# A 8192 x 8192 transpose: loads that split the rows of a chunk into even and odd halves

## The chip, the cores and the metric

The kernel runs on one core of one Trainium2 chip. Its time is the device time of one execution in microseconds. The time before is the median of three runs.

## The reference

```python
def setup_inputs():
    return {"x": np.random.randn(8192, 8192).astype(np.float32)}

def reference(x):
    return np.transpose(x)
```

An fp32 matrix of 268.4 MB is read once, and its transpose of the same size is written once.

## The kernel before

Each of the matrix's 8192 rows is 32 KB long. The work is cut into 128 chunks. A chunk is 128 rows by 4096 columns (`J = S * P`, 32 blocks of 128 columns), so 2 MB; the 64 chunks (`CH`) of the left half of the columns come first, then the 64 of the right half. Partition p of the chunk's buffer holds row p of the chunk, 16 KB of it in one piece.

One chunk passes through four stages:

- **Load.** `load(t)` issues one transfer from `x` into one of three buffers (`ins`, `NIN = 3`). The first three loads are issued on the SP queue, all later ones on the ACT queue. A load adds 16 to `s_ld[k]` of its buffer when it has landed.
- **Transposes.** `transposes(k)` on TensorE does 32 transposes of 128 x 128 against `ident`, with the data as the stationary side, into the two PSUM tensors `pss[0]` and `pss[1]` (16 blocks each). A group q of four transposes takes every fourth column of 512, so that four neighbouring output rows come to lie in one partition. TensorE begins a chunk when `s_ld[k]` is 18: 16 from the load and one from each copying engine, which says that the previous chunk's PSUM is free. It signals `s_pe` four times a chunk.
- **Copies.** ScalarE (ACT) copies `pss[0]` and VectorE (DVE) copies `pss[1]` into `regs`, a ring of nine regions in SBUF. A region collects the same q over eight successive chunks (`W = 8`), which makes 1024 neighbouring columns of the output, 4 KB for each output row.
- **Store.** When a region is full, `store(q, e, t)` writes it to `out` in one transfer of 2 MB, on the ACT queue. In the steady state one region closes per chunk. Before a region is used again, the copying engine waits for its last store (`s_st[r]`).

The order on ACT is written out by hand in the loop over `chunks`: the copies of chunk t, then a wait for the first signal of TensorE in chunk t+1 (by then both engines' copies of t are done), then the store that closed in t, then `load(t + NIN)`. So the store of t and the load of t+3 are issued one after the other, shortly after the load of t+1 has landed. The copies of chunk t+1 on ACT stand behind them.

`wide_dma` builds a transfer directly from the two access patterns that it is given, so that the source and the destination may be cut into pieces differently (stores read 16 KB from a partition and write it as four rows of 4 KB). `physical` writes the pattern down as it stands, and puts a count of 1 into a pattern of two dimensions. `dma_start` is the ordinary way, used for the loads and for the first transfer of a queue.

The diff touches the making of `ident` on GpSimd (POOL), `load`, one wait of VectorE, and one wait of TensorE.

Of the kernel before, what the change touches and what calls it, by code (L numbers as in the profile page):

```python
# [8 lines left out]
def physical(ap):  # L9


    t = ap.tensor
    dims = [list(d) for d in ap.ap]
    if len(dims) == 2:
        dims.insert(1, [dims[1][1], 1])
    return mybir.PhysicalAccessPattern(
        ap=dims,
        offset=ap.offset,
        dtype=ap.dtype,
        memref=t.name,  # L20
        memsetref=t.name + "_set",
    )


def wide_dma(nc, eng, queue, out, in_):


    return eng.add_instruction(
        mybir.InstDMACopy(
            mode="Copy",  # L30
            name=nc.get_next_instruction_name(),
            engine=eng.engine,
            ins=[physical(in_)],
            outs=[physical(out)],
            queue=queue,
        )
    )
# [3 lines left out]
def kernel(  # L41
# [13 lines left out]
    nc = tc.nc  # L55
    P = 128
# [8 lines left out]
    NIN = 3  # L65
    NREG = 9
    CH = N // P
    J = S * P

    with tc.tile_critical():  # L70
        nc.alloc_sbuf_tensor("pad", [P, 32], dt)
        ident = nc.alloc_sbuf_tensor("ident", [P, P], dt).ap()
        ins = [nc.alloc_sbuf_tensor(f"in{k}", [P, J], dt).ap() for k in range(NIN)]
        SIZE = B * W * P
# [4 lines left out]
        s_id = nc.alloc_semaphore("s_id")  # L79
        s_ld = [nc.alloc_semaphore(f"s_ld{k}") for k in range(NIN)]  # L80
# [3 lines left out]

        nc.gpsimd.memset(ident, 0.0).then_inc(s_id, 1)  # L85
        nc.gpsimd.wait_ge(s_id, 1)
        nc.gpsimd.affine_select(  # L87
            out=ident,
            in_=ident,
            compare_op=mybir.AluOpType.not_equal,  # L90
            fill=1.0,
            base=0,
            pattern=[[-1, P]],
            channel_multiplier=1,
        ).then_inc(s_id, 1)
        nc.vector.sem_inc(s_ld[0], 1)
        nc.scalar.sem_inc(s_ld[0], 1)

        chunks = [(s, c) for s in range(M // J) for c in range(CH)]

        def load(t):
            s, c = chunks[t]
            (nc.sync if t < NIN else nc.scalar).dma_start(
                out=ins[t % NIN], in_=x[c * P:(c + 1) * P, s * J:(s + 1) * J]
            ).then_inc(s_ld[t % NIN], 16)

# [16 lines left out]
        T = len(chunks)  # L125
        assert T % NIN == NIN - 1
        pe = [nc.tensor.engine]
        nc.tensor.wait_ge(s_id, 2)

        turn = nc.alloc_registers("turn", engines=pe)  # L130
        nc.regs_mov(turn, 0)
# [11 lines left out]
        for t in range(NIN):  # L143
            load(t)
# [9 lines left out]
        def store(q, e, t):  # L154
# [7 lines left out]
            for s, a, z in parts:  # L162
                rows = (z - a) * P
                j0 = s * J + q * B * P
                dst = out[j0:j0 + B * P, a * P:a * P + rows]
# [19 lines left out]
        for t, (s, c) in enumerate(chunks):  # L185
            closed = []
            for e in range(2):
                eng = (nc.scalar, nc.vector)[e]
# [4 lines left out]
                for q in range(e * NH, (e + 1) * NH):  # L193
# [14 lines left out]
                    base = r * SIZE + B * P * sum(z - a for _, a, z in parts[:k])  # L208
# [52 lines left out]
            if t + NIN < T:  # L261
                if not closed:
                    nc.scalar.wait_ge(s_pe, (t + 1) * NH)
                load(t + NIN)
# [32 lines left out]
```

## Time and profile before

| | |
|---|---|
| time, median of 3 runs | 1261.94 us (1261.61 to 1261.95) |
| span of the profiled execution | 1260.4 us |
| moved | 536.95 MB, 426 GB/s over the span |
| PE busy | 739.0 us (59%), 4096 matmuls |
| DVE busy | 302.0 us (24%) |
| ACT busy | 253.5 us (20%) |
| transfers | 128 loads of 2 MB, 142 stores of 256 KB to 2 MB |

The profile is one execution on the chip. Busy times are those of the compute engines; the issue of a transfer isn't counted as busy. The span is also shown in 40 equal slices: a digit is the busy share of a slice in tenths (9 is 90% or more), the row DMA is the mean busy share of the 16 DMA engines, and the row GB/s is what they moved. The rows on queues give packets, MB, and the time that the packets took as a share of 16 engines' span: q10 is ACT's queue, q1 is SP's. In the groups, the part behind the bar is busy time and the mean of one instruction, then the idle time ahead of them and what ended it.

### The profile page before, as it was taken

The numbers are of one execution on the slowest core, as the hardware profiler recorded it, in microseconds if no ns is written. First come the engines' busy times: TensorE is split into PE (matmuls) and PEld (weight loads), VectorE is DVE, ScalarE is ACT, GpSimd is POOL, SyncE is SP. The second block draws the span as 40 slices with busy tenths as digits, with TensorE's granted clock in tenths as the row PEclk, the third lists the DMA queues.
The fourth block names the chain that finished last, engine by engine and source line by source line (L and its number), as shares of the span: only waits on it lengthen the run. The fifth ranks groups of instructions, "written<-read, shape, count | busy, mean of one in ns | idle before, by whom it ended". The sixth has DMA issues, their size and how long they took to land. (4 is left out here: it accounts for less than half of the span.)

```text
span 1260.4 us, 9367 instructions
## 1 busy us (share of the span) xinstructions
PE 739.0 (59%) x4096; PEld 718.4 (57%) x4096; DVE 302.0 (24%) x250; ACT 253.5 (20%) x257; POOL 0.7 (0%) x6
## 2 busy tenths in 40 slices
PE   5656556565566655565556656566565655665561
PEld 5556556565556655565555656565565655665561
DVE  2322222222222222222222222222222222222220
ACT  3212211122111211122111211121111211121110
POOL 0000000000000000000000000000000000000000
PEclk9886876868777777778687786867777687777776
DMA  9999999999999999999999999999999999999998
GB/s 383 429 422 426 425 430 431 426 431 431 427 430 431 428 428 431 428 429 432 427 422 426 429 429 425 431 429 428 430 428 428 431 428 429 429 429 429 429 431 376
DMA packets 39271, 536.95 MB, mean 426 GB/s; under 512 B 4320, under 2 KB 4832, under 8 KB 6240
## 3 DMA queue, kind: packets, MB, share of 16 engines
q10 hardware_dynamic: 38832, 530.60, 99.0%
q1 hardware_dynamic: 432, 6.29, 1.2%
q14 instruction: 6, 0.05, 0.0%
q8 instruction: 1, 0.02, 0.0%
HBM read 268.44 MB, written 268.44 MB: 426 GB/s over the span
## 5 line engine op out<-in xcount | busy, mean ns | idle before, releaser
L117 PE MATMUL ps<-ident,in 128*128 128x128 f32 x4096 | 739.0, 362 | 493.5 <-PEq L113 493.5
L117 PEld LDWEIGHTS ps<-ident,in 128*128 128x128 f32 x4096 | 718.4, 220 | 513.9 <-issue 513.9
L241 DVE COPY regs<-ps 128x512 f32<-128x512 f32 (+3 forms) x250 | 302.0, 1246 | 932.1 <-PE ps L117 932.1
L241 ACT COPY regs<-ps 128x512 f32<-128x512 f32 (+3 forms) x256 | 252.2, 1016 | 978.8 <-PE ps L117 760.8
L241 ACT ACT_TABLE_LOAD x1 | 1.3, 1283 | 1.0 <-SPq L70 1.0
L87 POOL TENSOR_SCALAR_AFFINE_SELECT ident<-ident 128x128 f32<-128x128 f32 x1 | 0.3, 293 | 0.2 <-POOL ident L85 0.2
L85 POOL MEMSET ident<- 128x128 f32 x1 | 0.2, 204 | 0.5 <-SPq L70 0.5
L281 POOL MEMSET const-bfloat16-1.0<- 128x1 bf16 x1 | 0.1, 102 | 0.0
L281 POOL MEMSET const-uint8-127<- 128x1 uint8 x1 | 0.1, 102 | 0.0
L281 POOL MEMSET const-float32-0.0<- 128x1 f32 x1 | 0.1, 99 | 0.2 <-issue 0.2
L281 POOL MEMSET const-float32-1.0<- 128x1 f32 x1 | 0.1, 99 | 0.0
## 6 DMA issues: line engine op xcount, KB each, us to landing
in<-in_x_dram ACTq DMA_DIRECT2D x125, 2048.0 KB, 16.8
out_dram<-regs ACTq DMA_DIRECT2D x114, 2048.0 KB, 12.6
out_dram<-regs ACTq DMA_DIRECT2D x4, 1792.0 KB, 11.1
in<-in_x_dram SPq DMA_DIRECT2D x3, 2048.0 KB, 11.7
out_dram<-regs ACTq DMA_DIRECT2D x4, 1536.0 KB, 12.5
out_dram<-regs ACTq DMA_DIRECT2D x4, 1280.0 KB, 11.5
out_dram<-regs ACTq DMA_DIRECT2D x4, 1024.0 KB, 11.1
out_dram<-regs ACTq DMA_DIRECT2D x4, 768.0 KB, 12.3
```

The lines of the kernel that those rows point to most:

```text
L85: nc.gpsimd.memset(ident, 0.0).then_inc(s_id, 1)
L87: nc.gpsimd.affine_select(out=ident, in_=ident, compare_op=mybir.AluOpType.not_equal, fill=1.0, base=0, pattern=[[-1, P]], channel_multipl ...
L117: tr = nc.tensor.transpose(pss[e][:, (g * B + b) * P:(g * B + b + 1) * P], ins[k][:, q * B * P + b:(q + 1) * B * P - B + b + 1:B], ident,)
L241: cp = nc.scalar.copy(out=o, in_=i) if e == 0 else nc.vector.tensor_copy(out=o, in_=i)
L281: nc = _bacc.Bacc("TRN2", target_bir_lowering=False, num_devices=1)
```

## The change

The 128 rows of a chunk are put into the partitions in another order: the even rows into partitions 0 to 63, the odd ones into 64 to 127. On the side of `x` the load's pattern becomes 2 x 64 rows x 4096 values, with 32 KB between the two halves and 64 KB between the rows of a half; on the side of the buffer it is 128 partitions as before. These loads go through `wide_dma`. The first load on SP is issued as two ordinary transfers of 64 rows each, with a semaphore of its own (`s_l0`) for the second, which VectorE waits for ahead of its first increment. `ident` becomes the permutation that undoes the order: row p of it has its one at column 2p for p below 64, and at column 2(p - 64) + 1 above, so the transposes come out in the order of `x`. Stores, copies and the hand-written order are the same.

```diff
+    H = 2
+    L = P // H
...
-        nc.gpsimd.affine_select(
-            out=ident,
-            in_=ident,
-            compare_op=mybir.AluOpType.not_equal,
-            fill=1.0,
-            base=0,
-            pattern=[[-1, P]],
-            channel_multiplier=1,
-        ).then_inc(s_id, 1)
+        for h in range(H):
+            nc.gpsimd.affine_select(
+                out=ident[h * L:(h + 1) * L, :],
+                in_=ident[h * L:(h + 1) * L, :],
+                compare_op=mybir.AluOpType.not_equal,
+                fill=1.0,
+                base=h,
+                pattern=[[-1, P]],
+                channel_multiplier=H,
+            ).then_inc(s_id, 1)
+        s_l0 = nc.alloc_semaphore("s_l0")
+        nc.vector.wait_ge(s_l0, 16 * (H - 1))
         nc.vector.sem_inc(s_ld[0], 1)
         nc.scalar.sem_inc(s_ld[0], 1)
...
         def load(t):
             s, c = chunks[t]
-            (nc.sync if t < NIN else nc.scalar).dma_start(
-                out=ins[t % NIN], in_=x[c * P:(c + 1) * P, s * J:(s + 1) * J]
-            ).then_inc(s_ld[t % NIN], 16)
+            src = x[c * P:(c + 1) * P, s * J:(s + 1) * J].rearrange("(l h) j -> h l j", h=H)
+            if t == 0:
+                for h in range(H):
+                    nc.sync.dma_start(out=ins[t][h * L:(h + 1) * L], in_=src[h]).then_inc(s_ld[0] if h == 0 else s_l0, 16)
+            else:
+                eng, queue = (nc.sync, "qSPDynamicHW") if t < NIN else (nc.scalar, "qActDynamicHW")
+                wide_dma(nc, eng, queue, ins[t % NIN], src).then_inc(s_ld[t % NIN], 16)
...
-        nc.tensor.wait_ge(s_id, 2)
+        nc.tensor.wait_ge(s_id, 1 + H)
```

## The prediction

> **What bounds the kernel now.** I read the page first, its slices before its sums: 40 slices show whether one resource is full all the way through or each stage has its own limit.
>
> ```profile
> span 1260.4 us, 9367 instructions
> PE 739.0 (59%) x4096; PEld 718.4 (57%) x4096; DVE 302.0 (24%) x250; ACT 253.5 (20%) x257; POOL 0.7 (0%) x6
> ...
> DMA  9999999999999999999999999999999999999998
> GB/s 383 429 422 426 425 430 431 426 431 431 427 430 431 428 428 431 428 429 432 427 422 426 429 429 425 431 429 428 430 428 428 431 428 429 429 429 429 429 431 376
> DMA packets 39271, 536.95 MB, mean 426 GB/s; under 512 B 4320, under 2 KB 4832, under 8 KB 6240
> ...
> q10 hardware_dynamic: 38832, 530.60, 99.0%
> q1 hardware_dynamic: 432, 6.29, 1.2%
> ```
>
> The DMA row is full in every slice but the last; the busiest compute engine, PE, is busy for 59%. So this is a transfer-bound kernel, and the only thing that can move its time much is what the 16 DMA engines move, how fast, and how evenly they share it.
>
> Two numbers come out of these rows. First the rate of one engine. The middle slice value is 429 GB/s, or 429 / 16 = 26.81 GB/s each. From the busy time of q10 it is 530.60 MB / (0.990 x 16 x 1260.4 us) = 26.58, and the best slice gives 432 / 16 = 27.0. Second, how one transfer is shared out. On q1 there are three loads of 128 rows each (the SP issues below), and 432 = 3 x (128 + 16): 128 data packets of 16 KB and 16 tiny ones. The tiny ones are the semaphore writes, and they come once per part of a transfer.
>
> ```profile
> in<-in_x_dram ACTq DMA_DIRECT2D x125, 2048.0 KB, 16.8
> out_dram<-regs ACTq DMA_DIRECT2D x114, 2048.0 KB, 12.6
> out_dram<-regs ACTq DMA_DIRECT2D x4, 1792.0 KB, 11.1
> in<-in_x_dram SPq DMA_DIRECT2D x3, 2048.0 KB, 11.7
> ...
> out_dram<-regs ACTq DMA_DIRECT2D x4, 256.0 KB, 12.1
> ```
>
> There are 128 loads and 142 stores (114, and seven smaller sizes of 4 each), so 270 transfers; 270 x 16 = 4320, exactly the packets under 512 B. Every transfer of this kernel runs in 16 parts, one on each engine.
>
> Is 26.8 GB/s what one engine can do, or its sixteenth of something shared? The stretches tell:
>
> ```profile
> core 0: us, PE busy (x) PEld busy (x) DVE busy (x) ACT busy (x) POOL busy (x), PEclk, DMA share, GB/s
> 0.00:60.00 60.00, 36.76 (x256) 35.66 (x256) 17.33 (x27) 17.92 (x24) 0.70 (x6) 0.94 0.97 405
> 1140.00:1200.00 60.00, 36.01 (x201) 35.04 (x200) 14.13 (x12) 11.70 (x12) 0.00 (x0) 0.76 1.01 430
> 1200.00:1261.00 61.00, 21.31 (x119) 20.64 (x117) 9.68 (x12) 8.60 (x16) 0.00 (x0) 0.67 0.94 398
> ```
>
> In the two end stretches fewer engines are busy, yet a busy one moves no more: 405 / 16 / 0.97 = 26.1 and 398 / 16 / 0.94 = 26.5 GB/s, against 26.6 in the full stretch. A shared limit would have let the rest go faster. I take it as the engine's own rate.
>
> **The change, part by part.** *The load's shape.* Before, a load names 128 rows of 4096 values on the HBM side and 128 partitions on the SBUF side. After it, for every chunk but the first, the HBM side is 2 (odd or even) x 64 rows x 4096 values, and the SBUF side still 128 partitions. The bytes and the 16 KB rows are the same; the outermost count of the HBM side is 2 instead of 128. [...] Before, 128 and 128 could be cut in 16. Cut along its outermost count, the HBM side now yields two parts: even rows (partitions 0 to 63) and odd rows (64 to 127). I forecast that each of these loads runs on two engines, 64 rows on each.
>
> [...]
>
> The sum then goes by the two engines that carry all loads. A load is 128 x 16,384 B = 2.097 MB, so 1.049 MB for each of the two. Bytes on such an engine: 127 loads x 1.049 = 133.17 MB; the first chunk, loaded by two 64-row transfers whose outermost counts are 64 and 64 and which still split in 16, 0.13 MB; its sixteenth of the stores, whose shapes don't change, 268.44 / 16 = 16.78 MB. Together 150.08 MB, where before it carried 536.95 / 16 = 33.56 MB. At 26.81 GB/s that is 5598 us; at 27.0 it is 5559, at 26.58 it is 5646. I take the middle, since it is the long full stretch that resembles what follows.
>
> What else lies on the path is the start and the end, and whether the two engines ever run dry between.
>
> ```profile
> 0.94 1.32 SPq L103 DMA_DIRECT2D in<-in_x_dram  x3
> ...
> 1.38 0.29 POOL L87 TENSOR_SCALAR_AFFINE_SELECT ident<-ident 128x128 f32<-128x128 f32 x1 [0.23 <-POOL ident L85]
> 8.37 5.34 PEld L117 LDWEIGHTS ps<-ident,in 128*128 128x128 f32 x32 [8.37 <-issue]
> ...
> 1227.04 5.45 PE L117 MATMUL ps<-ident,in 128*128 128x128 f32 x32 [4.51 <-PEq L113]
> ...
> 1233.38 15.33 ACTq L28 DMA_DIRECT2D out_dram<-regs  x5
> ```
>
> Start: the first load's 2.10 MB take 4.9 us at 429 GB/s and are in by 8.37, so the engines start about 3.5 us in. End: from the start of the last transposes to the end of the span are 1260.4 - 1227.0 = 33.4 us, in which eight stores of 256 to 2048 KB (36 x 256 KB, 9.44 MB) take 22.0 us that the sum already has; up to 11.4 us remain. 5598 + 3.5 + 11.4 = 5613 us of span against today's 1260.4. The median of the three runs shown is 1261.9, 1.5 us over that span; less some of the end's 11.4, which earlier stores cover, I say 5610 us.
>
> *Do the two engines run dry?* The steady state of before:
>
> ```profile
> 610.77 6.28 PE L117 MATMUL ps<-ident,in 128*128 128x128 f32 x32 [3.69 <-PEq L113]
> 612.75 0.55 ACTq L28 DMA_DIRECT2D out_dram<-regs  x1
> 613.34 0.61 ACTq L103 DMA_DIRECT2D in<-in_x_dram  x1
> 613.98 2.05 ACT L241 COPY regs<-ps 128x512 f32<-128x512 f32 x4 [7.72 <-issue]
> 617.08 2.48 DVE L241 COPY regs<-ps 128x512 f32<-128x512 f32 x4 [7.49 <-PE ps L117]
> ```
>
> The transposes of chunk t+1 start when its load has landed; 2 us later ACT issues the store of t and the load of t+3. At that moment the load of t+2 still waits in the two engines' rings, 1.049 MB or 39.1 us of work each. From a landing to the next issue pass 2.57 us (610.77 to 613.34), and the copies are done by 617.08 + 2.48, 8.8 us after it. The rings hold over four times that, so no chunk exposes anything: a period is 39.1 + 0.131 / 26.81 = 4.9 for the store's share, 44.0 us, and everything else hides in it. The copies into a reused register also wait for the store of two chunks earlier; that store stands in the ring right behind the load that just landed, so it is in 4.9 us later.
>
> ACT may be held at the issue itself: in the end rows above five stores take 15.33 us to issue instead of 0.55 each, since others are still outstanding. A load now puts 64 rows into one ring where it put 8, so ACT will be held more often, with its own copies behind it, and through them (the next transposes wait for the copies) PE. [...]
>
> *The rest* is off the path.
>
> ```profile
> L117 PE MATMUL ps<-ident,in 128*128 128x128 f32 x4096 | 739.0, 362 | 493.5 <-PEq L113 493.5
> ```
>
> Two affine selects of 64 partitions for one of 128: another 0.3 us on POOL, 6 us before PE needs the matrix. A fourth issue on SP, 1.32 / 3 = 0.4 us. DVE waits for the second half of load 0 before its first increment; nothing but its copies of chunk 0 stands behind it, and those need the same data. TensorE does the same 4096 transposes, with a permutation in place of the identity: same shape, same count, 362 ns each, on an engine that will be busy a seventh of the time. Its bounds are nothing either way.
>
> **Rivals.**
> *A. Still 16 parts (not slower).* The partition side alone decides the split, which has 128 as before. Then every engine keeps 33.56 MB and the time stays at 1262 us; where the new row order suits the HBM better, the gain ends at the best slice, 536.95 MB / 432 = 1243 us plus some 12 at the ends, 1255; a poorer order might give the worst inner slice, 422, hence 1284. For it: the partitions alone make up the SBUF side, and all 270 transfers ran in 16. Against it: all of these had at least 128 outermost on both sides, so none could have shown otherwise, and a two-row-block source can't be cut in 16 along its outermost count. It decides if the semaphore packets of a load remain 16.
>
> *B. Two parts, but not always the same two engines.* If successive loads took different pairs, the two loads in flight would overlap: a period of about half of 44.0 us, 22 us, 128 x 22 + 15 = 2830 us. Nothing in the profile shows which engines a small split would take.
>
> *C. The rings run dry.* If ACT were held until a ring is empty, each chunk would add what lies between landing and next issue, 2.6 us, up to the whole 8.8 us: 128 x 2.6 = 330 or 128 x 8.8 = 1130 us, so 5940 to 6740 us. Against it: the end rows show ACT let go while transfers are still under way, with the DMA share of that stretch at 0.94.
>
> **How the numbers follow.** Two engines, fed without a gap: 0.87. A: 0.07, of which faster 0.03, the same 0.03 and slower 0.01. B: 0.03. C: 0.03. A measurement of this kernel can tell about 0.2% from no change. Faster 0.03, same 0.03, slower 0.94. The time is the first case's, 5610. Its own bounds are 5559 + 3.5 = 5560 and 5646 + 15 = 5660; both rates were read from sixteen busy engines, so I go some 2 to 4% beyond them for two that work almost alone: 5450 to 5850. That leaves out A, B and C, 0.13 together.
>
> **What would show it.** Right: q1 with 2 x (64 + 16) + 2 x (128 + 2) = 420 packets (448 if all loads ran in 16 parts); packets under 512 B down by 127 x 14 and up by 16, to 2558; a mean DMA share of some 22% and 536.95 MB / 5611 = 96 GB/s in every slice; chunks 44 us apart on PE; a load landing some 80 to 90 us after its issue and a store some 50, both set by the two rings; PE, DVE and ACT idle nearly throughout, with a few tenths of a microsecond per matmul as now. Wrong: 448 packets on q1 and a full DMA row (A), periods of 22 us (B), or gaps between the landing of one load and the next that grow past 44 us with nothing moving (C). A period of another length at 420 packets would mean that one engine nearly alone has another rate than 26.8 GB/s.

## The result, and the profile after

| | before | after |
|---|---|---|
| time, median | 1261.78 us (4 runs, 1261.39 to 1261.95) | 5576.93 us (4 runs, 5576.74 to 5576.97) |
| ratio | | 4.419 (4.414 to 4.425) |
| span of the profiled execution | 1260.4 us | 5575.2 us |
| moved, rate over the span | 536.95 MB, 426 GB/s | 536.95 MB, 96 GB/s |

The page of the changed kernel, the rows that answer to those of before:

```profile
span 5575.2 us, 9370 instructions
PE 759.5 (14%) x4096; PEld 738.8 (13%) x4096; DVE 301.9 (5%) x250; ACT 250.1 (4%) x257; POOL 1.0 (0%) x7
...
PEclk6655555555555555555555555555555555555555
DMA  2122222222222222222222222222222222222223
GB/s 69 83 92 93 107 93 93 94 93 107 94 94 93 94 97 103 93 93 93 93 107 93 93 93 93 103 97 93 93 94 95 105 93 94 93 93 107 93 93 151
DMA packets 37509, 536.95 MB, mean 96 GB/s; under 512 B 2558, under 2 KB 3070, under 8 KB 4478
...
q10 hardware_dynamic: 37082, 530.59, 22.3%
q1 hardware_dynamic: 420, 6.29, 0.4%
...
out_dram<-regs ACTq DMA_DIRECT2D x114, 2048.0 KB, 46.5
```

The same bytes are moved, and the compute engines are busy for about as long as before. What changed is the DMA row: from nine tenths or more in all slices but the last to about two, though the kernel waits for hardly anything but transfers. A mean over 16 engines says 22.3% both when all are busy a fifth of the time and when a few are busy all the time. The packet counts point to the second. q1 holds 420 packets, 2 x (64 + 16) + 2 x (128 + 2): the two loads of the new shape there end in two semaphore writes each instead of 16. Over the whole program the packets under 512 B fall from 4320 to 2558, which is 127 x 14 less and 16 more.

The timeline shows the start, the steady state with its period, and the last chunk (L28 is the line of `wide_dma`, which issues both loads and stores):

```profile
13.87 5.39 PE L126 MATMUL ps<-ident,in 128*128 128x128 f32 x32 [13.87 <-PEq L122]
...
2829.52 5.54 PE L126 MATMUL ps<-ident,in 128*128 128x128 f32 x32 [38.44 <-PEq L122]
2831.51 4.71 ACTq L28 DMA_DIRECT2D out_dram<-regs  x2
...
2836.25 4.85 ACTq L28 DMA_DIRECT2D in<-in_x_dram  x1
2841.13 2.05 ACT L250 COPY regs<-ps 128x512 f32<-128x512 f32 x4 [50.07 <-issue]
...
2873.26 5.82 PE L126 MATMUL ps<-ident,in 128*128 128x128 f32 x32 [38.20 <-PEq L122]
2875.25 2.93 ACTq L28 DMA_DIRECT2D out_dram<-regs  x2
...
5541.80 6.12 PE L126 MATMUL ps<-ident,in 128*128 128x128 f32 x32 [37.89 <-PEq L122]
```

The last chunk starts on PE at 5541.80, 62 chunks after the one at 2829.52: 43.75 us per chunk. In that time an engine that carries half of a load and a sixteenth of the stores moves 72 packets of 16 KB, so one each 607.6 ns, or 26.96 GB/s. The trace's own packet records agree: the median 16 KB packet takes 611 ns before and after. Between 20 and 5500 us, fewer than two data packets are in flight for less than 1 us in all, and for 88% of the time there are just two. So two engines are as fast as ever and do not pause; the others have little to do. That it is always the same two is read from the period: other pairs in turn would have shortened it.

### The profile page after: what moved, and what is told of

It reads as the page before. It is cut to its first block, busy times and chain, and to the rows that moved or that the text cites. A ratio compares the mean times of both kernels' runs of the same rounds, so it can differ in the third digit from the quotient of the medians.

```text
span 5575.2 us, 9370 instructions
## 1 busy us (share of the span) xinstructions
PE 759.5 (14%) x4096; PEld 738.8 (13%) x4096; DVE 301.9 (5%) x250; ACT 250.1 (4%) x257; POOL 1.0 (0%) x7
## 2 busy tenths in 40 slices
DMA packets 37509, 536.95 MB, mean 96 GB/s; under 512 B 2558, under 2 KB 3070, under 8 KB 4478
## 3 DMA queue, kind: packets, MB, share of 16 engines
q10 hardware_dynamic: 37082, 530.59, 22.3%
## 5 line engine op out<-in xcount | busy, mean ns | idle before, releaser
L126 PE MATMUL ps<-ident,in 128*128 128x128 f32 x4096 | 759.5, 370 | 4788.4 <-PEq L122 4788.4
L126 PEld LDWEIGHTS ps<-ident,in 128*128 128x128 f32 x4096 | 738.8, 221 | 4808.9 <-issue 4808.9
## 6 DMA issues: line engine op xcount, KB each, us to landing
out_dram<-regs ACTq DMA_DIRECT2D x114, 2048.0 KB, 46.5
```

Source lines behind the costliest of these rows:

```text
L126: tr = nc.tensor.transpose(pss[e][:, (g * B + b) * P:(g * B + b + 1) * P], ins[k][:, q * B * P + b:(q + 1) * B * P - B + b + 1:B], ident,)
```

## The experiments

**Is it the outermost count or the row order?** Each kernel here changes the load alone (and the permutation where rows move). The first keeps the old order and the identity, but names the source as two halves:

```diff
-            (nc.sync if t < NIN else nc.scalar).dma_start(
-                out=ins[t % NIN], in_=x[c * P:(c + 1) * P, s * J:(s + 1) * J]
-            ).then_inc(s_ld[t % NIN], 16)
+            src = x[c * P:(c + 1) * P, s * J:(s + 1) * J]
+            if t == 0:
+                nc.sync.dma_start(out=ins[t], in_=src).then_inc(s_ld[t], 16)
+            else:
+                src = src.rearrange("(h l) j -> h l j", h=2)
+                ...
+                wide_dma(nc, eng, queue, ins[t % NIN], src).then_inc(s_ld[t % NIN], 16)
```

> Loads name the source as 2 x 64 rows as in the change, but in the old order: rows 0 to 63, then 64 to 127, with the identity. Bytes and order are those of before; only the outermost count is 2. If the outermost count sets the number of parts: two engines carry all loads but the first, 127 x 64 + 8 + 1024 = 9160 packets of 16 KB, at the 607 ns that the changed kernel's period of 43.7 us gives for 72 packets 5560 us, and 15 at the ends: 5575 us, q1 with 144 + 2 x 130 = 404 packets. If the order of the rows (odd and even 32 KB apart, the permutation) is what costs: 1262 us, q1 432 packets.

It took 5572.51 us (one run), with 404 packets on q1. Rows, addresses and permutation are those of before, and the whole loss is there. The second differs from it in one thing, `"(l h) j -> l h j"`, a source of 64 x 2 rows:

> The same building of the load with a source of three counts, but the other way round: 64 x 2 rows, in the old order, with the identity. If the outermost count decides, 64 allows sixteen parts: 1262 us within 0.2%, q1 432 packets, loads of before in every respect. If a load with one count more on the source side is slow by itself: far above, up to 5577 us.

It took 1261.99 us, ratio 1.0001 (0.9992 to 1.001). So neither one more count in the source nor the way these transfers are built costs anything that these runs can tell. The outermost count does: 5572.51 us with 2, 1261.99 with 64. The page of each:

```profile
DMA packets 37493, 536.95 MB, mean 96 GB/s; under 512 B 2542, under 2 KB 3054, under 8 KB 4462
...
q1 hardware_dynamic: 404, 6.29, 0.3%
```

```profile
DMA packets 39271, 536.95 MB, mean 426 GB/s; under 512 B 4320, under 2 KB 4832, under 8 KB 6240
...
q1 hardware_dynamic: 432, 6.29, 1.2%
```

**Does the time follow the count?** The change with other counts: `H = 4`, `H = 8`, `H = 16`, with the permutation to match. For 8 and more, a transfer of 16 KB opens the SP queue and all chunks are loaded alike.

> The change with every fourth row in the same quarter: the source is 4 x 32 rows. By the outermost count, four engines carry the loads: 127 x 32 + 8 + 1024 = 5096 packets x 607 ns = 3093 us, and 15: 3108 us; a period of (32 + 8) x 0.607 = 24.3 us. If loads of this shape were slow for another reason (the row order, the way they are built), the time would stay near 5577 us or not follow the count.

> Every eighth row together, source 8 x 16 rows; the first chunk is loaded in the same way, behind a small transfer of 16 KB that opens the queue. By the outermost count eight engines carry the loads: 128 x 16 + 1024 = 3072 packets x 607 ns = 1865 us, and 15: 1880 us; a period of 14.6 us. Another reason: no such number.

> Every sixteenth row together, source 16 x 8 rows. By the outermost count all sixteen engines carry 8 rows of each load: 2048 packets x 607 ns = 1243 us, and 18: 1262 us, as before. [...]

| parts of a load | expected, us | measured, us |
|---|---|---|
| 2 (the change) | 5575 | 5576.93 |
| 4 | 3108 | 3129.7 (one run) |
| 8 | 1880 | 1914.8 (one run) |
| 16 (source of 16 x 8 rows) | 1262 | 1638 to 1820 (4 runs) |

Four and eight parts follow the count within 1 and 2%. The small excess was not isolated, but some packets are slow: 241 and 567 of the 30,977 packets of 16 KB took over 1000 ns, against 46 before. Sixteen parts do not follow. That is a miss, though all engines took part: the packets under 512 B are 4464, which is 16 for each of 271 transfers and the 128 short rows of the opening one. The slices of that kernel, and two stretches in the columns of the prediction's (DMA share and GB/s last), show how it is slow:

```profile
DMA  9999999999999999999999999999999999999998
GB/s 207 282 304 418 424 429 426 407 370 336 317 302 302 307 306 314 317 322 328 317 315 319 326 319 319 318 319 317 314 317 322 321 320 320 315 317 320 315 317 341
...
q10 hardware_dynamic: 38832, 530.60, 98.2%
```

```profile
165.00:330.00 165.00, 99.49 (x527) 96.94 (x528) 37.05 (x22) 31.35 (x32) 0.00 (x0) 0.72 1.01 421
900.00:1100.00 200.00, 89.24 (x480) 86.81 (x480) 36.26 (x22) 29.62 (x32) 0.00 (x0) 0.70 1.01 321
```

The engines are busy without a gap in both stretches, at 421 GB/s in one and 321 in the other. In this execution 53% of the 16 KB packets take under 640 ns, and 21% over 1100, about twice the normal. That looks as if two engines shared something that both use at some times and not at others; this is a guess, and no trace shows it.

**What is it: the row order, or where in SBUF the engines write?** Two more groups of runs. First the source as 16 x 8 rows again, but in the old order; and sixteen parts from 32 x 4 reordered rows:

> Source as 16 x 8 rows in the old order, identity: sixteen parts, cut along a count of 16 instead of 128, and no reordering. Where it equals the run with 16 x 8 reordered rows, the order of the rows is worth nothing and any difference to 1262 us is that of the cut. If neither matters: 1262 us within 0.2%.

> One transfer per load with the source as 32 x 4 rows (every thirty-second row together), permutation to match. The outermost count allows sixteen parts. By the engine rate 1262 us, plus 1 for the small transfer that opens the queue. If row order matters at HBM: 1255 to 1284 us.

The first took 1744 us (1716 to 1801, 6 runs), with nothing reordered. The second took 1262.82 us, ratio 1.001 (1.0 to 1.0019), with every row moved, which is about the 1 us expected for the opening transfer. So these orders of the rows are worth nothing that the runs can tell, and the miss lies in the cut along a count of 16; counts of 32, 64 and 128 run at the full rate (1262.82, 1261.99 and 1261.78 us).

Then the change's own row order with all engines, by two transfers of 64 rows:

```diff
...
+            eng = nc.sync if t < NIN else nc.scalar
+            for h in range(H):
+                eng.dma_start(out=ins[t % NIN][h * L:(h + 1) * L], in_=src[h]).then_inc(s_ld[t % NIN], 16)
...
-            nc.tensor.sem_inc(s_ld[k], -18).wait_op(s_ld[k], 18, "sem-ge")
+            nc.tensor.sem_inc(s_ld[k], -34).wait_op(s_ld[k], 34, "sem-ge")
```

> The row order of the change and its permutation, but each load as two transfers of 64 rows to 64 partitions, issued one behind the other; each has 64 outermost on both sides and runs in sixteen parts. This tells what the row order is worth with all engines. By the engine rate: 2048 packets of 16 KB per engine as before, 127 more issues of 0.6 us on ACT beside the transfers, 16 more small packets a load: 1262 us, at most 0.3% over. If the order of the rows in HBM costs or gains, 1255 to 1284 us as in rival A. A transfer of 64 partitions writes half of the partitions at a time; should that hold the engines back, packets get longer and the time goes above.

It took 1753 us (1645 to 1842, 6 runs). Even the fastest run lies far outside what was expected of the row order; the last sentence of the expectation, on half of the partitions, is what is left. Its two controls keep the old order and the two transfers, into `buf[h * 64:(h + 1) * 64]` with rows to match, and into every second partition, `bass.AP(buf.tensor, buf.offset + h * J, [[2 * J, 64], [1, J]])`:

> Each load as two transfers of 64 rows, the first to partitions 0 to 63, the second to 64 to 127, rows in the old order, identity. The same as the run with odd and even rows in two transfers, without the reordering. If two engines that write into the same group of partitions share its way in, these loads stay slow whatever the rows: 1640 to 1850 us, with half of the 16 KB packets at about twice 0.61 us. If the odd-even order is what made that run slow: 1262 us.

> Each load as two transfers of 64 rows again, but each to every second partition, so that one transfer spans all 128; rows in the old order, each transfer reads every second row (64 KB apart, as in the change). If the half of the partitions is what holds the engines back: 1262 us, at most 0.5% over, since 16 more small packets and one more issue a load lie beside the rest. If transfers of 64 rows, or reading every second row, are slow by themselves: 1640 us or more.

Halves: 1838 us (1774 to 1869, 4 runs). Every second partition: 1266.19 us, ratio 1.0031 (1.0014 to 1.0049), although each of its transfers reads every second row. Queue rows of the odd-even run, of the halves and of every second partition:

```profile
span 1840.1 us, 9497 instructions
...
q10 hardware_dynamic: 40832, 530.60, 98.7%
```

```profile
span 1808.7 us, 9495 instructions
...
q10 hardware_dynamic: 40832, 530.60, 98.6%
```

```profile
span 1264.3 us, 9495 instructions
...
q10 hardware_dynamic: 40832, 530.60, 99.0%
```

All three have the same packets on q10 and full engines. A busy engine moves 530.60 MB / (0.987 x 16 x 1840.1 us) = 18.3 GB/s in the first, 18.6 in the second and 26.5 in the third. With the halves, 37% of the 16 KB packets take over 1100 ns, against 0.1% with every second partition. Reading every second row is slow into halves and fast into every second partition. So here it is the set of partitions that one transfer writes that slows the engines.

What the engines meet there, no run shows: that two of them share a way into a group of partitions, as the expectation for the halves supposes, stays a guess that the doubled packets (37% with the halves) do not contradict. No trace shows which partitions an engine writes, so why 16 x 8 is slow (1638 to 1820 us) and 32 x 4 is not (1262.82 us) stays open.

## Why the prediction was right

*The split.* The step that carried it, two parts along the outermost count, holds by packets (420 and 2558, both as forecast), by time, and by the control that keeps the old rows (5572.51 us). The other counts agree: with sources of 2, 4, 8 and 16 parts the packets under 512 B are 2558, 2844, 3441 and 4464, where one semaphore write for each part of a load and 16 for every other transfer, with the rows of the opening transfer in the last two, make 2558, 2844, 3440 and 4464. The 150.08 MB of the sum rest on two terms that no run of before shows: that a count of 2 makes two parts, and that all loads go to the same two engines. The runs showed the first by these packets and the second by the period of 43.75 us.

*The rate.* 26.81 GB/s per engine was a little low: with two engines nearly alone it is 26.96. 150.08 MB at that rate are 5566 us instead of 5598. The ends took 5575.2 - 5566 = 9 us instead of 15. The forecast of 5610 us lies 0.6% over the time; most of that is the rate.

*The rings.* By a ring the prediction means the packets that wait at one engine; how many it holds, no run shows. The two engines never ran dry, as forecast (fewer than two data packets in flight for less than 1 us in all, as above), and ACT was held at the issue, as forecast. What holds it there, no run shows either. The row of the loads' issues in the changed kernel, with shortest, median and longest in ns:

```profile
L28 ACTq DMA_DIRECT2D in<-in_x_dram x125: 560/2297/22152, 19.3 to 5456.9; - x125
```

The longest took 22 us, and single stores up to 39 us. In the timeline above, two stores and a load hold ACT for 9.6 us, and its copies begin 11.6 us after the transposes instead of 3.2 (613.98 - 610.77 before). Yet the next chunk starts 43.74 us after this one: while ACT is held, the two engines have work queued. A store landed 46.5 us after its issue, where some 50 were forecast. The page has no time to landing for loads of two parts, but the trace bounds it: the load issued at 2836.25 fills the chunk that TensorE begins at 2917.05, 80.8 us later. Over the chunks from the ninth on this is 81 to 88 us, with a median of 85, as forecast (80 to 90).

*The first chunk.* Here the text was wrong with little consequence. It has TensorE begin when load 0 has landed, as before at 8.4 us; it began at 13.87. Its two transfers of 64 rows go to one half of the partitions each, the case found slow above: in these 14 us the median 16 KB packet took 1282 ns. The controls agree, since TensorE begins at 13.68 with the halves and at 8.57 with every second partition. The two engines had the next loads in their rings meanwhile, so little was lost: `halves_in_order`, whose first load is whole, is 4.4 us faster.

*The rivals.* A (still sixteen parts) falls with the 420 packets; and had it held, no row order tried here gains at HBM (1262.82 us with 32 x 4 rows, 1266.19 where each transfer reads every second row). B (other pairs of engines) would have given a period of 22 us, where 43.75 is measured. C (dry rings) would show gaps beyond 44 us with nothing moving. Only the first two gaps between chunks are clearly longer, 50.5 and 73.5 us, and all but 0.02 us of them has at least two data packets in flight. TensorE begins the chunk after them only 8 us later, which fits two loads, one on the SP queue and one on ACT's, that shared the engines.

*What a mend would bring.* The odd-even order itself was run with all engines in one form alone, two transfers by halves, and there it costs 30 to 46%. Two other forms run at the full rate: 32 x 4 rows, another order, at 1262.8 us, and every second partition, which reads every second row but leaves each row in its old place, at 1266.2 us. No run was clearly faster than before, whose engines already move a 16 KB packet in 611 ns without a gap.

## What to carry to other kernels

Before rearranging the access pattern of a transfer, look at the outermost count of the HBM side. The runs here lowered it, and it decided over how many engines the transfer spread: with counts of 8, 4 and 2 the kernel took 1914.8, 3129.7 and 5576.93 us instead of 1261.78, so a reshaping that names the same bytes can leave most engines idle. In the profile, count the packets under 512 B per transfer, since a mean DMA share of 22% hides two engines that are full. And in a kernel like this one, spread the partitions of one transfer over all 128, with an outermost count that ran at the full rate (32, 64 or 128, at 1262 to 1263 us): sixteen engines busy without a gap took 30 to 48% longer when a transfer wrote one half of the partitions, or was cut from a count of 16.

## What the runs showed of the hardware that was not expected

Sixteen parts are not always equal to sixteen parts: cut from an outermost count of 16, the transfers ran at 302 to 429 GB/s in the slices of one execution after its second, and the time varied from 1638 to 1820 us between runs, where single loads cut from 32, 64 or 128 gave 1262 to 1263 us. And in the change, where TensorE was busy for 14% of the span instead of 59%, the granted clock was lower (0.56 in the mean, 0.755 before); its matmuls took 370 ns in the mean instead of 362.
